# The branch around a rare path put directly behind one expert's last down products, with the next experts' rows and first weights prepared ahead of it

## The chip, the cores and the metric

The kernel runs on one core of a Trainium2 chip, in one launch. The time is device time in microseconds. The kernel before takes 2640.4 us, the median of three runs (2638.09, 2640.43, 2640.40). The engines are PE (TensorE, matrix products), DVE (VectorE), ACT (ScalarE), POOL (GpSimd) and SP (SyncE, which issues the transfers here). Each engine has its own instruction stream, and the engines wait for one another by semaphores. In the views a name with q behind it (PEldq, DVEq) stands for an engine's sequencer, which hands instructions to the engine and carries out loads of registers and branches itself.

## The reference

Two transformer blocks on 256 tokens of width 1024, in fp32, followed by a second program part of the same kind. The change touches the mixture of experts in the second layer, which is followed by a dense FFN:

```python
def moe_swiglu(h, w_router, w_gate, w_up, w_down):
    t = h.reshape(bsz * seq, d)                       # 256 x 1024
    logits = (t @ w_router).astype(jnp.float32)
    top_vals, top_idx = lax.top_k(logits, TOP_K)      # 2 of 8 experts
    top_w = jax.nn.softmax(top_vals, axis=-1)
    gates = jnp.sum(jax.nn.one_hot(top_idx, N_EXPERTS) * top_w[..., None], axis=1)
    out = jnp.zeros_like(t)
    for e in range(N_EXPERTS):
        out = out + gates[:, e:e + 1] * swiglu(t, w_gate[e], w_up[e], w_down[e])
    return out.reshape(bsz, seq, d)
```

Each expert has a gate and an up matrix of 1024 x 2816 and a down matrix of 2816 x 1024.

## The kernel before, in words

**Products.** Every fp32 matrix is split into a high and a low part: ACT casts the high part (`whi`, L156), DVE subtracts it (`wlo`, L159), each for pieces of 128 x 1024. A product is then three matmuls, high by high, high by low and low by high. Weights stream in transfers of 1 MB that SP issues (L168) into nine buffers, five named `raw` and four named `more`. There are five buffers of `whi` and four of `wlo`.

**The experts.** `moe_main` runs four experts per call. `gather` (L1260, with `xh` on ACT L1265 and `xl` on DVE L1266) picks the rows of two experts at a time: 32 matmuls with a matrix of zeros and ones (`g`, L1221). For an expert the gate and up products follow in six column blocks (L1283 to L1285), then the transposed `fh` and `fl`, then the down products in two chunks of 512 columns (L1307 to L1309; the last expert has chunks of 512, 256 and 256). A chunk's result is scaled by the row's gate into `yh` (ACT, L1311) and `yl` (DVE, L1312), and eight matmuls per 512 columns scatter it back to the tokens (L1317, L1318, "the sums" below), which DVE adds to the residual `xT` (L606). `rowwise` (L1231, L1233) makes the transposed `gt` for the sums and the gates `gr`.

**The branch.** The gathered rows hold at most 128 tokens an expert. Where one has more, `moe_rest` computes the rest in a general path, under `tc.If(n > P)` (L1211); the count `n` is loaded from `mi` (L1210). With these inputs the path is not run. The branch stands between the fourth and the fifth expert. Every engine loads the count into a register and branches by itself, and behind the branch it raises its semaphore by what the skipped path would have raised it.

**The order.** Loops emit the program, and a scheduler orders each engine's instructions by their dependencies and by estimated times, so an instruction may be moved across others of its engine, but not across the branch. Tiles of a pool are given free at its end: `p` is the pool `moe` (all of the experts), `q` is `moe_e` or `moe_f` (one call of `moe_main`). Behind the experts the FFN begins: `gg` (DVE, L556) is a product of two scales, `hl` (ACT L559, DVE L560) is the scaled `xT` in two parts, and L183 to L185 are the FFN's products. `sq` and `part` (L256, L259, L574) are for the norm.

## Time and profile before

| | |
|---|---|
| median of three runs | 2640.4 us |
| the profiled execution | 2640.62 us |
| its span | 2638.8 us |
| PE busy | 2568.5 us (97%) |
| DVE busy | 1973.1 us (75%) |
| ACT busy | 1560.9 us (59%) |
| POOL busy | 6.4 us (0%) |
| HBM read | 604.50 MB |
| mean granted clock | 0.982 |

The span runs from the first to the last instruction of the core; 1.8 us of the execution lie around it. PE is busy nearly throughout, and in the page's chain of work that ended last it holds most of the path, so what counts are the stretches in which PE stands and those in which its granted clock is at half. [...] Durations of matmuls overlap their neighbours, since they are pipelined: a matmul of 128x512 shows 0.39 us but the next one starts 0.23 us later.

### The profile page before, as it was taken

The numbers are of one execution on the slowest core, as the hardware profiler recorded it, in microseconds if no ns is written. First come the engines' busy times: TensorE is split into PE (matmuls) and PEld (weight loads), VectorE is DVE, ScalarE is ACT, GpSimd is POOL, SyncE is SP. The second block draws the span as 40 slices with busy tenths as digits, with TensorE's granted clock in tenths as the row PEclk, the third lists the DMA queues.
The fourth block names the chain that finished last, engine by engine and source line by source line (L and its number), as shares of the span: only waits on it lengthen the run. The fifth ranks groups of instructions, "written<-read, shape, count | busy, mean of one in ns | idle before, by whom it ended". The sixth has DMA issues, their size and how long they took to land.

```text
span 2638.8 us, 46342 instructions
## 1 busy us (share of the span) xinstructions
PE 2568.5 (97%) x18529; PEld 2358.6 (89%) x18529; DVE 1973.1 (75%) x3012; ACT 1560.9 (59%) x2191; POOL 6.4 (0%) x27
## 2 busy tenths in 40 slices
PE   7989998989999998999999999999999999999998
PEld 5779998978888887888878999989999999989998
DVE  5777668686999997999889765677665666677664
ACT  4444436674778876877777444675444444675443
POOL 0000000000000000000000000000000000000000
PEclk8989999998999999999999999999999999999999
DMA  9768766516999997999998557525556657525552
GB/s 310 240 219 273 266 195 224 160 65 211 350 362 350 353 378 281 345 359 348 342 362 280 175 184 218 160 65 166 186 175 193 186 176 221 155 66 175 179 181 89
DMA packets 453646, 608.62 MB, mean 231 GB/s; under 512 B 21563, under 2 KB 314448, under 8 KB 453424
## 3 DMA queue, kind: packets, MB, share of 16 engines
q1 hardware_dynamic: 453062, 605.26, 68.9%
q8 instruction: 147, 2.41, 0.4%
q0 software_dynamic: 176, 0.26, 0.1%
q14 instruction: 75, 0.61, 0.1%
q10 hardware_dynamic: 186, 0.07, 0.0%
HBM read 604.50 MB, written 1.05 MB: 229 GB/s over the span
## 4 chain that ended last, share of the span: by engine, by line
PE 59%; DVE 1%; issue 0%; ACT 0%; DVEq 0%
PE acc L183 10%; PE acc L184 10%; PE acc L185 10%; PE s L185 3%; PE s L184 3%; PE s L183 3%; PE acc L1284 3%; PE acc L1283 3%; PE acc L1285 3%; PE acc L1308 2%; PE acc L1307 1%; PE acc L1309 1%; PE s L320 1%; PE po L320 1%; PE sm L911 1%; DVE wlo L159 1%
## 5 line engine op out<-in xcount | busy, mean ns | idle before, releaser
L156 ACT CAST whi<-raw 128x1024 fp32r<-128x1024 f32 x816 | 838.4, 1038 | 710.4 <-PE acc L184 425.2
L159 DVE TENSOR_TENSOR wlo<-raw,whi 128x1024 fp32r<-128x1024 f32 x816 | 972.7, 1204 | 288.0 <-PE acc L185 202.3
L183 PE MATMUL acc<-hl,whi 128*128 128x256 f32 x2336 | 666.5, 286 | 1.9 <-ACT hl L307 1.1
L184 PE MATMUL acc<-hl,whi 128*128 128x256 f32 x2336 | 661.9, 283 | 1.7 <-DVE hl L560 0.8
L185 PE MATMUL acc<-hl,wlo 128*128 128x256 f32 x2336 | 660.5, 283 | 0.0
L183 PEld LDWEIGHTS acc<-hl,whi 128*128 128x128 f32 x2336 | 442.1, 189 | 4.9 <-ACT hl L307 1.4
L184 PEld LDWEIGHTS acc<-hl,whi 128*128 128x128 f32 x2336 | 441.9, 189 | 4.5 <-issue 1.5
L185 PEld LDWEIGHTS acc<-hl,wlo 128*128 128x128 f32 x2336 | 441.7, 189 | 0.6
L159 DVE TENSOR_TENSOR wlo<-more,whi 128x1024 fp32r<-128x1024 f32 x238 | 282.6, 1219 | 20.0 <-PE acc L1284 6.1
L1284 PE MATMUL acc<-wlo,xh 128*128 128x512 f32 (+1 forms) x768 | 288.3, 376 | 0.8
L1283 PE MATMUL acc<-whi,xh 128*128 128x512 f32 (+1 forms) x768 | 288.8, 378 | 0.0
L1285 PE MATMUL acc<-whi,xl 128*128 128x512 f32 (+1 forms) x768 | 286.0, 373 | 0.0
L156 ACT CAST whi<-more 128x1024 fp32r<-128x1024 f32 x238 | 243.7, 1047 | 42.7 <-PE acc L1285 26.9
L183 PE MATMUL s<-hl,whi 128*128 128x256 f32 x880 | 248.5, 282 | 0.0
L184 PE MATMUL s<-hl,whi 128*128 128x256 f32 x880 | 248.5, 282 | 0.0
L185 PE MATMUL s<-hl,wlo 128*128 128x256 f32 x880 | 248.4, 282 | 0.0
L1284 PEld LDWEIGHTS acc<-wlo,xh 128*128 128x128 f32 x768 | 144.4, 188 | 28.1 <-DVE wlo L159 4.5
L1283 PEld LDWEIGHTS acc<-whi,xh 128*128 128x128 f32 x768 | 144.3, 188 | 25.8
L1285 PEld LDWEIGHTS acc<-whi,xl 128*128 128x128 f32 x768 | 144.3, 188 | 25.1
L183 PEld LDWEIGHTS s<-hl,whi 128*128 128x128 f32 x880 | 166.3, 189 | 0.0
L184 PEld LDWEIGHTS s<-hl,whi 128*128 128x128 f32 x880 | 166.2, 189 | 0.0
L185 PEld LDWEIGHTS s<-hl,wlo 128*128 128x128 f32 x880 | 166.2, 189 | 0.0
(477 smaller groups left out, 4091.2 us busy)
## 6 DMA issues: line engine op xcount, KB each, us to landing
raw<-in_moe_w_gate_dram SPq DMA_DIRECT2D x50, 1024.0 KB, 7.0
raw<-in_moe_w_up_dram SPq DMA_DIRECT2D x48, 1024.0 KB, 6.7
raw<-in_ffn_wg_dram SPq DMA_DIRECT2D x44, 1024.0 KB, 5.4
raw<-in_ffn_wu_dram SPq DMA_DIRECT2D x44, 1024.0 KB, 5.4
raw<-in_moe_w_down_dram SPq DMA_DIRECT2D x42, 1024.0 KB, 6.9
more<-in_moe_w_up_dram SPq DMA_DIRECT2D x40, 1024.0 KB, 7.8
more<-in_moe_w_gate_dram SPq DMA_DIRECT2D x38, 1024.0 KB, 6.4
raw<-in_w_in_dram SPq DMA_DIRECT2D x38, 1024.0 KB, 5.3
```

The source lines that it names most:

```text
L156: i = nc.scalar.copy(hi, src[:, k0 : k0 + m])
L159: nc.vector.tensor_sub(lo, src[:, k0 : k0 + m], hi)
L183: mm(out, whi, xhi, start=first, stop=False, skip_group_check=True)
L184: mm(out, whi, xlo, start=False, stop=False, skip_group_check=True)
L185: mm(out, wlo, xhi, start=False, stop=last, skip_group_check=True)
L320: m = self.nc.tensor.matmul(o, w, x, start=start, stop=stop, skip_group_check=True)
L911: nc.tensor.transpose(ptp[:, b * P : (b + 1) * P], pe[:, b * P : (b + 1) * P], self.ident)
L1283: mm(a, xh[:, k], hi, start=k == 0, stop=False, skip_group_check=True)
L1284: mm(a, xh[:, k], lo, start=False, stop=False, skip_group_check=True)
L1285: mm(a, xl[:, k], hi, start=False, stop=k == 7, skip_group_check=True)
L1307: mm(a, fh[k], hi, start=k == 0, stop=False, skip_group_check=True)
L1308: mm(a, fh[k], lo, start=False, stop=False, skip_group_check=True)
```

## The change

The general path's branch is moved to directly behind the fourth expert's last down products: the eight sums of its second chunk (`sums`) are emitted behind the branch. `gather(4)`, which was emitted behind the branch, is emitted ahead of the fourth expert's down products, and the first two 1 MB loads of the fifth expert's gate matrix are split ahead of the branch (`self.pre`). Since these tiles are now used on both sides, `xh`, `xl`, `yh`, `yl` and `gt` come from `p` instead of `q`. The activation `tab` behind the branch is left out; the load of the count is emitted in the second expert's turn.

```diff
@@ -173,7 +174,8 @@
-            for k, (hi, lo) in enumerate(zip(*self.split(first.pop(0) if first else self.load(w, k0, nk, n0, n)))):
+            hl = self.pre.pop(0) if self.pre else self.split(first.pop(0) if first else self.load(w, k0, nk, n0, n))
+            for k, (hi, lo) in enumerate(zip(*hl)):
...
@@ -1205,14 +1207,14 @@
             split = 4
+            st = {"g": g, "rows": [], "back": [], "load": lambda: nc.values_load(mi[0:1, 0:1], min_val=0, max_val=T)}
             with tc.tile_pool(name="moe_e", bufs=1, reuse_waits="tile") as q:
-                self.moe_main(p, q, ht, pos, gates, first, 0, split, g)
-            n = nc.values_load(mi[0:1, 0:1], min_val=0, max_val=T)
-            with tc.If(n > P):
+                self.moe_main(p, q, ht, pos, gates, first, 0, split, st)
+            with tc.If(st["n"] > P):
...
@@ -1224,7 +1226,7 @@
-        gt = q.tile([P, T], dt, tag="gt", bufs=3, name=self.name("gt"))
+        gt = q.tile([P, T], dt, tag="gt", bufs=2, name=self.name("gt"))
...
@@ -1248,8 +1250,8 @@
-            xh, xl = (q.tile([P, KT, 2 * P], F32R, tag=s, bufs=1, name=self.name(s)) for s in ("xh", "xl"))
+            xh, xl = (p.tile([P, KT, 2 * P], F32R, tag=s, bufs=1, name=self.name(s)) for s in ("xh", "xl"))
...
@@ -1266,11 +1268,16 @@
-        nc.scalar.activation(q.tile([1, 1], F32, name="tab"), self.ones[:1, :1], AF.Silu)
-        g, rows = gather(e0)
-        back = []
+        if e0 == 0:
+
+            nc.scalar.activation(q.tile([1, 1], F32, name="tab"), self.ones[:1, :1], AF.Silu)
+            st["g"], st["rows"] = gather(e0)
+        else:
+            st["last"]()
+        g, rows, back = st["g"], st["rows"], st["back"]
         for e in range(e0, e1):
+            if e == 1:
+                st["n"] = st["load"]()
...
@@ -1291,13 +1298,13 @@
-                    back = [self.rowwise(q, g[:, :, b], gates, e + b, F32R) for b in range(2)]
+                    back = [self.rowwise(p, g[:, :, b], gates, e + b, F32R) for b in range(2)]
...
-            if not rows and e + 1 < e1:
+            if not rows and e + 1 < NE:
                 g, rows = gather(e + 1)
...
@@ -1307,16 +1314,25 @@
-                yh, yl = (q.tile([P, 512], F32R, tag=t, bufs=1, name=self.name(t))[:, :n] for t in ("yh", "yl"))
+                yh, yl = (p.tile([P, 512], F32R, tag=t, bufs=1, name=self.name(t))[:, :n] for t in ("yh", "yl"))
                 nc.scalar.activation(yh, a, AF.Identity, scale=gr)
                 v.scalar_tensor_tensor(yl, a, gr, yh, ALU.mult, ALU.subtract)
...
+                def sums(n0=n0, n=n, yh=yh, yl=yl, gt=gt, e=e):
...
+                if e + 1 == e1 < NE and n0:
+
+                    self.pre = [self.split(self.load(wg[e1], k0, 4, 0, 512)) for k0 in (0, 4)]
+                    st.update(g=g, rows=rows, back=back, last=sums)
+                else:
+                    sums()
...
@@ -1326,7 +1342,7 @@
-            r = q.tile([P, 8, 256], F32, tag="raw", bufs=2, name=self.name("oraw"))[:, :nk]
+            r = q.tile([P, 8, 256], F32, tag="raw", bufs=1, name=self.name("oraw"))[:, :nk]
```

PE at the branch. Of before, the rows from the fourth expert's last down product on; `s` is the result of a sum, the numbers tell tiles apart:

```order
L1309 MATMUL acc_10387<-whi_10500,fl_10243 128x512
L1317 MATMUL s_10514<-gt_8975,yh_10510 128x256 [waits Activation_49]
L1317 MATMUL s_10521<-gt_8975,yh_10510 128x256
L1318 MATMUL s_10514<-gt_8975,yl_10511 128x256 [waits DVE_49]
L1317 MATMUL s_10514<-gt_8975,yh_10510 128x256
L1318 MATMUL s_10514<-gt_8975,yl_10511 128x256
L1318 MATMUL s_10521<-gt_8975,yl_10511 128x256
L1317 MATMUL s_10521<-gt_8975,yh_10510 128x256
L1318 MATMUL s_10521<-gt_8975,yl_10511 128x256
L1210 TENSOR_LOAD mi [waits DVE_49]
L1211 COMPARE_AND_BRANCH
```

and of before, behind the not taken path:

```order
L1211 UNCONDITIONAL_BRANCH [waits PE_49]
L1260 MATMUL s_14624<-g_14617,hl_6776 128x256 [waits DVE_49]
L1260 MATMUL s_14624<-g_14617,hl_6776 128x256 x3
L1260 MATMUL s_14625<-g_14617,hl_6776 128x256 [waits DVE_49]
L1260 MATMUL s_14625<-g_14617,hl_6776 128x256 x3
```

Of after, PE's same place, with the first rows behind the path at the end:

```order
L1314 MATMUL acc_10460<-whi_10573,fh_10256 128x512
L1315 MATMUL acc_10460<-wlo_10574,fh_10256 128x512
L1316 MATMUL acc_10460<-whi_10573,fl_10257 128x512
L1210 TENSOR_LOAD mi [waits DVE_49]
L1213 COMPARE_AND_BRANCH
...
L1213 UNCONDITIONAL_BRANCH [waits PE_49]
L1326 MATMUL s_14680<-gt_8989,yh_10583 128x256 [waits DVE_49,Activation_49]
L1327 MATMUL s_14680<-gt_8989,yl_10584 128x256
L1326 MATMUL s_14680<-gt_8989,yh_10583 128x256
L1327 MATMUL s_14680<-gt_8989,yl_10584 128x256
L1290 MATMUL acc_14694<-whi_10589,xh_10265 128x512 [waits Activation_49]
```

The sums and the 32 matmuls of `gather(4)` have changed sides; behind the branch the sums come first, and the fifth expert's gate products directly behind them. The load of the count stands directly ahead of the branch in both.

DVE at the branch, of before from `yl` on:

```order
L1312 SCALAR_TENSOR_TENSOR yl_10511<-acc_10387,gr_8982,yh_10510 128x512 [waits Activation_49]
L159 TENSOR_TENSOR wlo_14702<-more_14699,whi_14701 128x1024 [waits DVE_49,DMAHW6_49,PE_49,Activation_49]
L606 SCALAR_TENSOR_TENSOR xT<-s_10514,mod_147,xT 128x256 [waits PE_49]
L606 SCALAR_TENSOR_TENSOR xT<-s_10514,mod_147,xT 128x256
L606 SCALAR_TENSOR_TENSOR xT<-s_10521,mod_147,xT 128x256 [waits PE_49]
L606 SCALAR_TENSOR_TENSOR xT<-s_10521,mod_147,xT 128x256
L159 TENSOR_TENSOR wlo_14706<-more_14699,whi_14705 128x1024 [waits DVE_49,Activation_49]
L1210 TENSOR_LOAD mi [waits DVE_49]
L1211 COMPARE_AND_BRANCH
```

and of after, with the two subtractions ahead of `yl`:

```order
L160 TENSOR_TENSOR wlo_10600<-more_10597,whi_10599 128x1024 [waits DVE_49,DMAHW6_49,PE_49,Activation_49]
L160 TENSOR_TENSOR wlo_10604<-more_10597,whi_10603 128x1024 [waits DVE_49,PE_49,Activation_49]
L1319 SCALAR_TENSOR_TENSOR yl_10584<-acc_10460,gr_8996,yh_10583 128x512 [waits Activation_49]
L1210 TENSOR_LOAD mi [waits DVE_49]
L1213 COMPARE_AND_BRANCH
```

The four additions to `xT` have gone behind the branch, and `yl` is the last instruction ahead of the load.

PE at the end of the last expert, where the FFN starts. Of before, from the last two down products on:

```order
L1308 MATMUL acc_18234<-wlo_18310,fh_17973 128x256
L1309 MATMUL acc_18234<-whi_18309,fl_17974 128x256
L183 MATMUL acc_18437<-hl_18347,whi_18440 128x256 [waits Activation_49]
L184 MATMUL acc_18437<-hl_18348,whi_18440 128x256 [waits DVE_49]
L185 MATMUL acc_18437<-hl_18347,wlo_18441 128x256
L183 MATMUL acc_18437<-hl_18347,whi_18440 128x256
...
L1317 MATMUL s_18335<-gt_16706,yh_18331 128x256 [waits Activation_49]
```

Of after:

```order
L1315 MATMUL acc_18232<-wlo_18308,fh_17971 128x256
L1316 MATMUL acc_18232<-whi_18307,fl_17972 128x256
L1326 MATMUL s_18333<-gt_16704,yh_18329 128x256 [waits Activation_49]
L1327 MATMUL s_18333<-gt_16704,yl_18330 128x256 [waits DVE_49]
L1326 MATMUL s_18333<-gt_16704,yh_18329 128x256
L1327 MATMUL s_18333<-gt_16704,yl_18330 128x256
L251 MATMUL sm_18384<-ones,part_18109 128x1 [waits DVE_49,PE_49]
L251 MATMUL sm_18384<-ones,part_18109 128x1
L185 MATMUL acc_18435<-hl_18345,whi_18438 128x256 [waits Activation_49]
L185 MATMUL s_18494<-hl_18345,whi_18497 128x256
```

Before, 25 FFN products stand between the last down product and the first of the last four sums. Now the sums come first, then two matmuls for the norm (L251), and the FFN's first product behind them.

ACT at the same place. Of before:

```order
L156 CAST whi_18444<-raw_18438 128x1024 [waits DVE_49,PE_49]
L559 ACTIVATE hl_18347<-xT,gg 128x256 [waits DVE_49,Activation_49]
L559 ACTIVATE hl_18347<-xT,gg 128x256 x3
L559 ACTIVATE hl_18347<-xT,gg 128x256 [waits DVE_49]
L156 CAST whi_18499<-raw_18497 128x1024 [waits DMAHW6_49,PE_49]
L156 CAST whi_18503<-raw_18497 128x1024 [waits PE_49,Activation_49]
L1311 ACTIVATE yh_18331<-acc_18234,gr_16713 128x256 [waits PE_49]
L256 ACTIVATE sq_18231<-xT 128x512 [waits DVE_49]
L559 ACTIVATE hl_18347<-xT,gg 128x256
```

Of after:

```order
L157 CAST whi_18497<-raw_18495 128x1024 [waits DMAHW6_49,DVE_49,PE_49]
L157 CAST whi_18501<-raw_18495 128x1024 [waits DVE_49,PE_49]
L1318 ACTIVATE yh_18329<-acc_18232,gr_16711 128x256 [waits PE_49]
L258 ACTIVATE sq_18229<-xT 128x512 [waits DVE_49]
L576 ACTIVATE sq_18372<-xT,colsb 128x256 x2
L157 CAST whi_18564<-raw_18562 128x1024 [waits DMAHW7_49,Activation_49]
L576 ACTIVATE sq_18376<-xT,colsb 128x256 [waits DVE_49]
L576 ACTIVATE sq_18376<-xT,colsb 128x256
L576 ACTIVATE part_18369<-xT,colsb 128x256 x2
L561 ACTIVATE hl_18345<-xT,gg 128x256 [waits DVE_49]
L561 ACTIVATE hl_18345<-xT,gg 128x256 x7
```

Before, the first five `hl` stand ahead of the last two casts and of the last `yh`. Now all eight stand behind them, behind `sq`, behind another cast and behind six activations of L576 (L574 before). On DVE `gg`, which `hl` reads, has likewise gone from ahead of the first FFN weights' subtraction to behind the last additions to `xT`.

## Rows read from the trace of the kernel before

**Rows 1.** Windows: stretch, length, busy by engine (PE, PEld, DVE, ACT, POOL), clock, DMA share, GB/s

```profile
1060.00:1440.00 380.00, 379.06 (x1888) 316.10 (x1887) 346.26 (x356) 288.67 (x327) 0.00 (x0) 1.00 0.99 345
```

**Rows 2.** Timeline of PE at the branch; start, duration, instruction, idle before and releaser

```profile
1032.56 0.40 PE L1309 MATMUL acc<-whi,fl 128*128 128x512 f32 x1
1033.74 0.50 PE L1317 MATMUL s<-gt,yh 128*128 128x256 f32 x2 [0.78 <-ACT yh L1311]
1034.52 0.38 PE L1318 MATMUL s<-gt,yl 128*128 128x256 f32 x1 [0.29 <-DVE yl L1312]
...
1035.22 0.28 PE L1318 MATMUL s<-gt,yl 128*128 128x256 f32 x1
1041.62 5.49 PE L1260 MATMUL s<-g,hl 128*128 128x256 f32 x24 [6.12 <-DVEq L1211]
```

**Rows 3.** Timeline of DVE at the branch

```profile
1033.72 0.75 DVE L1312 SCALAR_TENSOR_TENSOR yl<-acc,gr,yh 128x512 fp32r<-128x512 f32 x1 [1.41 <-ACT yh L1311]
1035.79 1.65 DVE L606 SCALAR_TENSOR_TENSOR xT<-s,mod,xT 128x256 f32<-128x256 f32 x4
```

**Rows 4.** Instructions of L1210, the load of the count: durations in ns, starts

```profile
L1210 PEldq TENSOR_LOAD <-mi x1: 484/484/484, 1034.5 to 1034.5; - x1
L1210 DVEq TENSOR_LOAD <-mi x1: 547/547/547, 1035.7 to 1035.7; - x1
```

**Rows 5.** Instructions of L1211, the branch: durations in ns, starts

```profile
L1211 POOLq EVENT_SEMAPHORE  x4: 17/42/43, 646.4 to 646.7; - x4
L1211 POOLq COMPARE_BRANCH  x1: 45/45/45, 642.5 to 642.5; - x1
...
L1211 PEldq COMPARE_BRANCH  x1: 6212/6212/6212, 1035.1 to 1035.1; - x1
L1211 DVEq COMPARE_BRANCH  x1: 72/72/72, 1036.3 to 1036.3; - x1
...
L1211 DVEq EVENT_SEMAPHORE  x1: 21/21/21, 1041.5 to 1041.5; - x1
```

**Rows 6.** Windows that begin with PE's resumption behind a gap, and the FFN's start

```profile
1041.62:1050.00 8.38, 8.38 (x45) 8.12 (x45) 3.37 (x8) 2.83 (x7) 0.00 (x0) 0.67 0.19 72
417.76:427.00 9.24, 9.24 (x57) 9.14 (x58) 7.93 (x24) 5.91 (x8) 0.00 (x0) 0.74 0.37 123
385.44:400.00 14.56, 14.56 (x87) 14.45 (x88) 11.38 (x22) 6.06 (x11) 0.00 (x0) 0.67 0.38 115
1440.00:1450.00 10.00, 9.17 (x77) 8.97 (x77) 9.72 (x16) 8.72 (x16) 0.00 (x0) 1.00 0.72 211
```

**Rows 7.** Timeline of PE, the first instruction behind two gaps

```profile
385.44 0.98 PE L287 MATMUL sm<-dg,ones 128*128 128x128 f32 x3 [2.69 <-DVE dg L286]
417.76 0.55 PE L183 MATMUL acc<-g,whi 128*128 128x256 f32 x1 [5.04 <-DVE bc L940]
```

**Rows 8.** Timeline of PE at the start of the FFN

```profile
1440.17 0.28 PE L1309 MATMUL acc<-whi,fl 128*128 128x256 f32 x1
1440.29 0.28 PE L183 MATMUL acc<-hl,whi 128*128 128x256 f32 x1
1441.39 0.39 PE L184 MATMUL acc<-hl,whi 128*128 128x256 f32 x1 [0.83 <-DVE hl L560]
```

**Rows 9.** Timeline of ACT at the start of the FFN

```profile
1440.00 1.98 ACT L156 CAST whi<-raw 128x1024 fp32r<-128x1024 f32 x2
1441.89 0.46 ACT L1311 ACTIVATE yh<-acc,gr 128x256 fp32r<-128x256 f32 x1
1442.25 0.61 ACT L256 ACTIVATE sq<-xT 128x512 f32<-128x512 f32 x1
1442.77 0.49 ACT L559 ACTIVATE hl<-xT,gg 128x256 fp32r<-128x256 f32 x1
1443.17 0.89 ACT L574 ACTIVATE sq<-xT,colsb 128x256 f32<-128x256 f32 x2
1443.97 1.98 ACT L156 CAST whi<-raw 128x1024 fp32r<-128x1024 f32 x2
```

## The prediction

> **What bounds the kernel now.** I read the windows of the experts first. Between 1060 and 1440 us PE works 379.06 of 380.00 us at full clock, while DVE works 346 and ACT 289 [rows 1]. So PE is the bound, and work moved between places where PE is fed changes nothing. What can change the time is a stretch in which PE stands, or runs at half clock. The PE timeline, read next, shows such a stretch at the branch.

> The last down product of the fourth expert begins at 1032.56 and ends at T = 1032.96 [rows 2]. PE waits for `yh` and `yl`, does the eight sums until 1035.50, and then stands 6.12 us until 1041.62 [rows 2]. From T to the resumption that is 8.66 us, of which the sums are eight steps of 0.116 us, 0.93 us (256 columns; the FFN rows 1440.17 and 1440.29 are one such step apart [rows 8]). So 7.73 us are lost, and a clock loss comes on top: the 8.38 us behind the resumption have a mean granted clock of 0.67, so 0.33 x 8.38 = 2.8 us [rows 6].

> What the wait is made of stands in the rows of L1210 and L1211. DVE's sequencer loads the count at 1035.7 (547 ns), which is just behind the end of the last sum at 1035.50, for which DVE's last two additions to `xT` wait. It compares at 1036.3, and the first event behind the branch comes at 1041.5 [rows 2 to 5]. PE's sequencer loads at 1034.5, when its last wait, that for `yl`, is met, and its branch holds it for 6212 ns from 1035.1 to about 1041.3 [rows 4, 5]. PE's first matmul is released by DVE's sequencer [rows 2]. So the chain is: the last wait ahead of an engine's branch is met, load and compare take 0.6 us, some 5.2 us pass before the next instruction, in sum 5.8 us on DVE. The sequencer doesn't wait for its engine: DVE's four additions run until 1037.44 [rows 3] while its sequencer is at the branch.

> **The change at the branch.** The sums and their additions are now behind the branch. DVE's last wait ahead of it is that of `yl` for `yh`. With the durations of before `yl` could start at 1033.72, T + 0.76 [rows 3]. The load then begins at T + 0.8 instead of T + 2.75, and with the same 5.8 us the event comes at T + 6.6 and PE resumes at T + 6.7 (before, 0.1 us lay between them). PE's own sequencer has its last wait ahead of T and ends its 6.7 us (484 ns and 6212 ns) at or before T + 6.7. All of PE's work that lay in the gap is now behind it: lost are 6.7 us instead of 7.73, a gain of 1.0 us.

> How long the 5.2 us are is not fixed. POOL's own branch shows 3.9 us (642.5 to 646.4) and PE's 6.2 [rows 5]. With 3.9 the resumption is at T + 5.4, a gain of 2.3, with 6.2 at T + 7.7, which is no gain. I take 5.2, DVE's own. [...]

> The gather's 32 matmuls move ahead of the branch into a stretch with no room on PE; they cost there what they no longer cost behind it. Before, 24 of them ran at half clock (5.49 us [rows 2]). Now the sums and the first gate products, which come behind the resumption, take that place, so the clock loss of 2.8 us stays as it is. The casts and subtractions of the first two loads (four pieces, 24 matmuls of 512 columns, twice 0.116 us each, 5.5 us) are a stock on which PE lives while ACT and DVE start again. The five `whi` buffers and the four of `wlo` were filled ahead of the branch before as well, by the scheduler. The load of the count stands directly ahead of the branch in both orders, so its earlier place in the text does nothing, and the dropped `tab` (0.20 us on ACT) was on no path. I cost these at nothing, since DVE has 9% and ACT 24% of free time in the experts [rows 1]; without that cover the gather's work on ACT and DVE would show as waits of PE ahead of T.

> **The change at the FFN.** The order shows a second difference, far from the branch. At the end of the eighth expert, 25 FFN products used to fill the time in which the last `yh` and `yl` are made. PE stood there for 0.83 us only, and the clock stayed at 1.00 [rows 6, 8]. Now PE has the sums, two small matmuls and then the FFN's first product, which waits for the first `hl`, and on ACT that stands behind much else.

> I follow ACT from T2 = 1440.45, the end of the last down product [rows 8], with the starts of before as the price of each step [rows 9]. The last cast ahead of `yh` needs a `whi` buffer that six matmuls from the end comes free, at T2 - 0.7; it takes 1.05 us (half of the pair's 1.98, plus its tail), so `yh` starts at T2 + 0.4. `yh` takes 0.36 until `sq` can start, `sq` 0.52, the first two L576 0.80, a cast 0.95, two more pairs of L576 0.80 each. That is 0.4 + 0.36 + 0.52 + 0.8 + 0.95 + 1.6 = 4.6, and `hl` takes 0.49, so it is done at T2 + 5.1. PE can start at 5.15. Of this the four sums are 0.47 us of work, so PE stands 4.7 us where it stood 0.83. **The loss is 3.85 us.** DVE's `gg` comes ahead of that: it is behind a subtraction, `yl`, two adds and two additions to `xT`, by about T2 + 3.8 as I estimate from a subtraction's 1.2 us and `yl`'s 0.75 at twice the width.

> A gap of that size was followed by half clock elsewhere. Behind the gap of 5.04 us at 417.76 the mean clock of the next 9.24 us was 0.74, so 2.4 us were lost; behind that of 2.69 us at 385.44 it was 0.67 over 14.56 us, so 4.8 us [rows 6, 7]. The lower end is nothing, as behind the 0.83 us [rows 6, 8]. I take 2.4, from the gap that is nearest in length.

> **The sum.** -1.0 at the branch, +3.85 and +2.4 at the FFN: +5.2 us. The profiled execution took 2640.62 us (a span of 2638.8 and 1.8 around it), 0.2 us above the median of 2640.4. So 2645.8 by the first and 2645.6 by the second; I predict 2645.6.

> **The rivals.**
> - *The clock holds at the FFN.* The 4.7 us are not one gap: four sums and two small matmuls lie in them. Then the time is 2640.4 - 1.0 + 3.85 = 2643.2. Against it: the 2.69 us gap was enough for a fall [rows 6, 7].
> - *The FFN's start is covered.* If ACT comes to its last casts earlier than I have it (in after it has five fewer `hl`, 2 us, to do ahead of them), `hl` could be early enough to hide most of the gap: at most the branch's gain is left, 2640.4 - 1.0 = 2639.4, or 2638.1 with the short branch. Against it: the buffers of `whi`, not ACT, hold those casts back, and the order forbids `hl` to pass them.
> - *The price is the full one, clearly slower.* The clock stays at half as long as behind 385.44, and the branch is as long as PE's own: 2640.4 + 0 + 3.85 + 4.8 = 2649.1. It decides if the FFN's first 9 us or so run at half. For it: of the two gaps measured the shorter one had the longer stretch [rows 6, 7].
> [...]
> [...]

> **How the numbers follow.** A difference under 0.2% (5.3 us) can't be told from none in a measurement of this kernel; the bounds are 2635.1 and 2645.7. The forecast has a chance of 0.50 with an own range of 2643.5 to 2647.5, and lies astride the upper bound: 0.26 of it within, 0.24 above. The clock that holds: 0.18, within. The covered start: 0.10, within. The full price: 0.15, above. Faster: 0.07, near the lower bound, of which 0.04 below it. So faster 0.04, the same 0.57, slower 0.39. The range of 2638.5 to 2650 leaves out the fast case and a part of the covered one, and takes in the upper ends of the clock and the branch.

> **What would show it.** In the trace after: DVE's sequencer loading the count some 0.8 us behind the last down product, and PE resuming 6.7 us behind it, with the sums first; a clock at half for some 5 us from there on, as before; no waits of PE in the fifth expert's gate products. At the FFN: PE idle for 4 to 5 us ahead of the first product of L185, released by `hl` of ACT (L561), and half clock behind it. The prediction is wrong if PE is fed there in under 2 us, if the branch's rows shorten by more than 2.5 us, or if new waits of PE show up in the experts.

## The result: slower by 0.53%, and the profile after

The changed kernel takes 2654.19 us (median of five runs, 2650.82 to 2658.46) against 2640.1 us (five runs). The ratio is 1.0053 with a 95% interval of 1.0043 to 1.0064, so 14 us slower; 2645.6 was forecast. The profiled execution took 2653.55 us with a span of 2651.4, which is 12.6 us over the span before.

The windows of the changed kernel, one of the experts as in [rows 1], one from PE's resumption at the branch, and one from the FFN's first product; the columns are those of [rows 1]:

```profile
1060.00:1440.00 380.00, 379.40 (x1854) 313.41 (x1853) 343.04 (x357) 285.69 (x319) 0.00 (x0) 1.00 0.98 342
1049.93:1058.00 8.07, 8.07 (x31) 6.81 (x32) 5.20 (x7) 2.94 (x3) 0.00 (x0) 0.75 0.08 24
1453.50:1462.00 8.50, 8.40 (x60) 8.39 (x61) 5.74 (x13) 5.21 (x12) 0.00 (x0) 0.81 0.29 93
```

In the experts PE is busy as before, at full clock (1.00). Its time looks the same, but it does less in it: 1854 matmuls in 380 us against 1888 (part of that is that the windows cover other instructions). So the steps themselves must be looked at. PE's timeline, the first and the last of 47 matmuls of 512 columns in a row, in the third expert's gate and up products, of the kernel before (in these rows the first name behind the arrow, `wlo`, is the moving operand and the second, `xh`, the stationary one, which PEld loads ahead of the matmul: the 128x128 load for the first of them runs 0.19 us from 859.74):

```profile
859.97 0.39 PE L1284 MATMUL acc<-wlo,xh 128*128 128x512 f32 x1
...
870.52 0.39 PE L1285 MATMUL acc<-whi,xl 128*128 128x512 f32 x1
```

and of the changed kernel:

```profile
863.01 0.40 PE L1291 MATMUL acc<-wlo,xh 128*128 128x512 f32 x1
...
873.74 0.39 PE L1292 MATMUL acc<-whi,xl 128*128 128x512 f32 x1
```

A step is the time from one matmul's start to the next one's. Before, 46 steps take 10.55 us, 0.2293 each; after, 10.73 us, 0.2333 each. Nothing waits there, no clock is below full, and the durations shown (0.39, 0.40) hardly tell. Over the experts' products, 512-column steps have these means (in us, all of them at full clock):

| | before | after |
|---|---|---|
| gate and up, all experts | 0.2294 | 0.2334 |
| down, experts 1 to 4 | 0.2299 | 0.2333 |
| down, experts 5 to 8 | 0.2297 | 0.2283 |

PE at the branch, after; the fence answers to [rows 2]:

```profile
1041.78 0.40 PE L1316 MATMUL acc<-whi,fl 128*128 128x512 f32 x1
1049.93 0.55 PE L1326 MATMUL s<-gt,yh 128*128 128x256 f32 x1 [7.75 <-DVEq L1213]
...
1051.56 0.41 PE L1327 MATMUL s<-gt,yl 128*128 128x256 f32 x1
1051.77 0.63 PE L1290 MATMUL acc<-whi,xh 128*128 128x512 f32 x1
```

The last down product ends at T = 1042.18, PE resumes at 1049.93, 7.75 us later, and the eight sums come behind it. Before, 8.66 us less 0.93 of sums were lost, 7.73. So the branch costs what it did. The loads of the count and the branches, after, which answer to [rows 4, 5]:

```profile
L1210 PEldq TENSOR_LOAD <-mi x1: 484/484/484, 1037.8 to 1037.8; - x1
L1210 DVEq TENSOR_LOAD <-mi x1: 545/545/545, 1042.9 to 1042.9; - x1
```

```profile
L1213 PEldq COMPARE_BRANCH  x1: 6233/6233/6233, 1038.4 to 1038.4; - x1
L1213 ACTq COMPARE_BRANCH  x1: 45/45/45, 1042.8 to 1042.8; - x1
L1213 DVEq COMPARE_BRANCH  x1: 72/72/72, 1043.6 to 1043.6; - x1
L1213 ACTq EVENT_SEMAPHORE  x1: 17/17/17, 1043.9 to 1043.9; - x1
...
L1213 PEldq EVENT_SEMAPHORE  x1: 51/51/51, 1044.7 to 1044.7; - x1
L1213 DVEq EVENT_SEMAPHORE  x1: 21/21/21, 1049.8 to 1049.8; - x1
```

DVE loads 0.76 us behind T, as forecast. But from its compare to its event 6.2 us pass, not 5.2. ACT needs 1.0 us where it had needed 5.2. PE's own branch starts 3.8 us ahead of T and is over at 1044.7, so DVE's is the one that PE waits for.

The FFN's start, first PE, which answers to [rows 8], then ACT, to [rows 9]:

```profile
1447.54 0.28 PE L1316 MATMUL acc<-whi,fl 128*128 128x256 f32 x1
1448.61 0.38 PE L1326 MATMUL s<-gt,yh 128*128 128x256 f32 x1 [0.79 <-ACT yh L1318]
1450.87 0.58 PE L1327 MATMUL s<-gt,yl 128*128 128x256 f32 x1 [1.88 <-DVE yl L1319]
...
1453.60 0.58 PE L185 MATMUL acc<-hl,whi 128*128 128x256 f32 x1 [0.60 <-ACT hl L561]
```

```profile
1447.14 1.05 ACT L157 CAST whi<-raw 128x1024 fp32r<-128x1024 f32 x1 [0.74 <-PE acc L1316]
1448.09 0.47 ACT L1318 ACTIVATE yh<-acc,gr 128x256 fp32r<-128x256 f32 x1
...
1451.44 0.91 ACT L576 ACTIVATE sq<-xT,colsb 128x256 f32<-128x256 f32 x2 [0.64 <-DVE part L261]
1452.26 0.89 ACT L576 ACTIVATE part<-xT,colsb 128x256 f32<-128x256 f32 x2
1453.06 3.29 ACT L561 ACTIVATE hl<-xT,gg 128x256 fp32r<-128x256 f32 x8
```

The first FFN product starts 5.78 us behind the last down product's end at 1447.82 (5.15 forecast), released by ACT's first `hl`. The 0.63 us more are about what ACT waits for DVE's `part` (0.64), which the forecast did not have. The half clock behind it (0.50 in windows of 1 us from 1453.60 to 1456.60, 0.81 over the 8.50 us of the third window) is 1.6 us.

**Where the 12.6 us are.** From start to start, summed over PE's matmuls between the first gate product and the last down product, and behind it:

| part | after less before, us |
|---|---|
| gate, up and down products, steps | +10.9 |
| the gather's matmuls (now at full clock, 1.00 from 940 to 1042) | -2.5 |
| the sums (now partly at half clock, 0.50 from 1050 to 1053) | +1.0 |
| steps over 0.45 us (waits), the branch's included | -1.7 |
| transposes and the row-wise matmuls | -0.4 |
| first 400 matmuls behind the last down product (53.8 against 48.6) | +5.2 |
| all the rest | +0.1 |

Of the 10.9 about 1 us is half clock that lay on the gather before. Some 10 us are longer steps, most of the loss, and the prediction had no such term.

### The profile page after: what moved, and what is told of

Same layout as the page of the kernel before. It is cut to its first block, busy times and chain, and to the rows that moved or that the text cites. A ratio compares the mean times of both kernels' runs of the same rounds, so it can differ in the third digit from the quotient of the medians.

```text
span 2651.4 us, 46351 instructions
## 1 busy us (share of the span) xinstructions
PE 2582.9 (97%) x18529; PEld 2364.4 (89%) x18529; DVE 1973.7 (74%) x3012; ACT 1562.6 (59%) x2190; POOL 6.4 (0%) x27
## 3 DMA queue, kind: packets, MB, share of 16 engines
HBM read 604.50 MB, written 1.05 MB: 228 GB/s over the span
## 4 chain that ended last, share of the span: by engine, by line
PE 59%; DVE 1%; ACT 0%; issue 0%; DVEq 0%
PE acc L185 10%; PE acc L186 10%; PE acc L187 9%; PE s L187 3%; PE s L186 3%; PE s L185 3%; PE acc L1291 3%; PE acc L1290 3%; PE acc L1292 3%; PE acc L1315 2%; PE acc L1314 2%; PE acc L1316 1%; PE s L322 1%; PE po L322 1%; PE sm L913 1%; DVE wlo L160 1%
## 5 line engine op out<-in xcount | busy, mean ns | idle before, releaser
L185 PE MATMUL acc<-hl,whi 128*128 128x256 f32 x2336 | 668.0, 286 | 1.9 <-ACT hl L309 1.1
L185 PEld LDWEIGHTS acc<-hl,whi 128*128 128x128 f32 x2336 | 443.1, 190 | 4.9 <-ACT hl L309 1.4
L157 ACT CAST whi<-more 128x1024 fp32r<-128x1024 f32 x238 | 244.5, 1048 | 60.3 <-PE acc L1292 37.9
L185 PE MATMUL s<-hl,whi 128*128 128x256 f32 x880 | 248.9, 283 | 0.0
L185 PEld LDWEIGHTS s<-hl,whi 128*128 128x128 f32 x880 | 166.8, 190 | 0.0
```

What stands on the lines that cost most here:

```text
L157: i = nc.scalar.copy(hi, src[:, k0 : k0 + m])
L185: mm(out, whi, xhi, start=first, stop=False, skip_group_check=True)
```

## The experiments

One thing that differs between the kernels in that stretch without touching an instruction is where the tiles lie. The built programs have the addresses: `xh` begins at byte 176352 of a partition before and 176320 after, `fh` at 196832 before, after at 203072 in the first call and at 203040 in the second (`tab`, 32 bytes with its padding, is only in the first). The split weights stay: `whi` begins at 76064 and `wlo` at 96544, both in steps of 4096. In the experts' products `xh`, `xl`, `fh`, `fl` are stationary, the weights move. All the comparisons are with the kernel before in runs on the same chip.

**Place alone, in the changed kernel (e1).** Instructions and order are the same on every engine.

```diff
+            p.tile([1, 1], F32, name="pad")          # first call, ahead of xh
             st["g"], st["rows"] = gather(e0)
         else:
+            q.tile([1, 1], F32, name="padf")         # second call, ahead of s and fh
             st["last"]()
```

> The changed kernel with 32 unused bytes ahead of xh and another 32 in the second call's pool, so that xh begins at byte 176352 of a partition instead of 176320 and fh at 203104; every instruction and its order are as in the changed kernel. Theory (place): PE's step of a 512-column matmul depends on whether its stationary tile begins at a multiple of 64 bytes; the gate products' mean step falls from 0.2334 to about 0.229 us, the down products' of experts 0 to 3 from 0.2333 to 0.229, and the time by 7 to 10 us to about 2645. Rival (order): the longer step comes from the new order or from the other engines' work beside it; then the step stays at 0.233 and the time at 2654.

2650.2 us, ratio 1.0038 (1.0026 to 1.0051); 1.0053 without the pads. The 47 matmuls of the third expert's gate and up products:

```profile
867.46 0.39 PE L1293 MATMUL acc<-wlo,xh 128*128 128x512 f32 x1
...
878.00 0.39 PE L1294 MATMUL acc<-whi,xl 128*128 128x512 f32 x1
```

46 steps in 10.54 us, 0.2291: the gate's long step is gone with 32 bytes. But `fh`, at 203104 now, has 0.2332 in the first call and 0.2334 in the second, where it had 0.2283, so a multiple of 64 isn't the rule, and part of the gain is lost: 1920 gate and up steps x 4.1 ns = 7.9 us less, and 462 down steps x 5.1 ns = 2.4 us more. That is 5.5 us net, where 7 to 10 were expected; by the medians 14.1 us over the kernel before became 10.9.

**The FFN's order alone (e2).** The shared tiles are in a pool of their own, at the same addresses.

```diff
+            sh = c.enter_context(tc.tile_pool(name="moe_x", bufs=1, reuse_waits="tile"))
-            st = {"g": g, ...
+            st = {"x": sh, "g": g, ...
-            xh, xl = (p.tile(
+            xh, xl = (st["x"].tile(       # yh, yl, gt, gr likewise
```

> The changed kernel with xh, xl, yh, yl, gt and gr in a pool of their own that lies at the same addresses as before, so that the FFN's first tiles overlap no pool that holds them. The order at the start of the FFN is that of the kernel before again (25 FFN products ahead of the last sums), the rest is as in the changed kernel. Theory (place, and FFN order apart): PE's wait at the FFN's start and the half clock behind it go, the steps stay long: 5 to 6 us faster than the changed kernel, about 2648.5. Rival (one cause: the FFN's start costs little): under 2 us faster.

2649.1 us, ratio 1.0036 (1.0023 to 1.0049). PE's only wait over 0.1 us at the FFN's start (engine, line, releaser; total, times, longest us):

```profile
PE acc L186 <- DVE hl L562: 0.7, 1, 0.7
```

The order is again that of the kernel before, the first 400 matmuls behind the last down product take 48.6 us as before, and the steps are long as in the changed kernel. So what moved `gg` and `hl` is the pool that the shared tiles belong to, and not their addresses. My reading is that the scheduler puts a tile that opens a region behind the last use of every pool that held the region, and that with `yl` and `gt` in `moe` this last use came later; no other run tests that rule.

**Both (e3).**

> Both edits: the pool of their own and the 32 bytes. Theory: the two gains add up, 13 us off the changed kernel, 2640 to 2641, what is left against the kernel before is the branch alone, a difference within 2 us. Rival: the branch's place itself costs more than its trace shows, and the time stays over 2645.

2645.6 us, ratio 1.0023 (1.0013 to 1.0034). The two gains add up (14.1 - 3.2 - 4.3 gives 6.6 over the kernel before, 6.2 measured), but the down products' step of 0.2333 stays in it, which the expectation had not. By the time alone the rival could stand (over 2645, since the branch's place costs more than its trace shows); e5 and e6 decide between the two.

**Place alone, in the kernel before (e4).** Unused bytes ahead of `xh`, 32 in the first call, 64 in the second; instructions and order as before.

```diff
+        for k in range(2 if e0 else 1):
+            q.tile([1, 1], F32, name=self.name("pad"))
         g, rows = gather(e0)
```

> The kernel before with 32 unused bytes ahead of xh in the first call of the experts (xh at byte 176384, fh at 196864, both multiples of 64) and 64 bytes in the second (176416 and 196896, both 32 past one); instructions and order as in the kernel before. Theory (place): experts 0 to 3 take the long step, 0.233 us, experts 4 to 7 stay at 0.227 to 0.229; 5 to 7 us slower than the kernel before, about 2646. Rival (order): both halves stay at 0.229 and the time at 2640.

2643.0 us, ratio 1.0013 (1.0004 to 1.0021). Experts 1 to 4 have steps of 0.2331 (gate) and 0.2333 (down), experts 5 to 8 0.2281 and 0.2278. Both halves are as the place theory said; from the steps 960 x 3.8 ns + 528 x 3.4 ns - 960 x 1.4 ns - 462 x 1.9 ns = 3.2 us, and 3.6 were measured. The 5 to 7 us expected were too many, since the second half became faster instead of staying as it was. The order rival falls.

**The good place in both (e5, e6).** `xh` at 176416 in both; `fh` at 203296 in e5 (on e2's pools), at 196896 in e6 (the kernel before with 64 unused bytes in each call).

> The changed kernel with the pool of its own for the shared tiles, and unused bytes so that xh begins at byte 176416 and fh at 203296 in both calls, both 32 past a multiple of 256, as in the fast half of the shifted kernel before. Theory (the step goes by the stationary tile's place within 256 bytes, 32 is fast): all 512-column steps of the experts at 0.228 us; against the version with both edits 0.0013 x 1920 and 0.005 x 1000, 7 us faster, about 2638. Rival (the step goes by whether the place is a multiple of 64): the gate products' step stays at 0.2293, the down products' falls to it, 2642.

> The kernel before, order unchanged, with 64 unused bytes ahead of xh in both calls: xh at 176416, fh at 196896, 32 past a multiple of 256. Theory (place): steps of 0.228 instead of 0.2293 and 0.2298, so 1.3 ns x 1920 and 1.9 ns x 1000, about 4 us faster than the kernel before, 2635.5. What the aligned changed kernel takes more or less than this one is the branch and nothing else: between -1 and +2 us. Rival (the place matters only where it is bad): 2639.5, as before.

2634.8 us, ratio 0.9979 (0.9970 to 0.9988), and 2635.9 us, ratio 0.9985 (0.9976 to 0.9994). The same 47 matmuls in e6:

```profile
860.52 0.39 PE L1286 MATMUL acc<-wlo,xh 128*128 128x512 f32 x1
...
870.95 0.39 PE L1287 MATMUL acc<-whi,xl 128*128 128x512 f32 x1
```

46 steps in 10.43 us, 0.2267. The means are 0.2276 to 0.2282 in both. e6 is 4.6 us under the kernel before, as expected (about 4). e5 came out lower than expected (2638): by the ratios it is 0.44%, 11.6 us, under e3, where 7 were expected and 8.4 follow from the steps measured; the intervals of the two are too wide to tell these apart. What is left between the two kernels is the branch's place: 1.2 us, with intervals that overlap, so no difference that these runs can tell. PE's wait at the branch in e5 and in e6 (there behind the sums):

```profile
PE s L1333 <- DVEq L1214: 8.0, 1, 8.0
```

```profile
PE s L1260 <- PEq L1211: 6.0, 1, 6.0
```

**Place or distance (e7).** On e6: the stationary tiles of the experts stay, the moving ones are moved by 32 bytes.

```diff
+        if not self.padded:
+            self.padded = self.pw.tile([1, 1], F32, name="padw")
         for s, b in (("whi", self.nhi), ("wlo", self.nlo)):
```

> The same as the aligned kernel before, but with 32 unused bytes ahead of the split weights too, so that the moving tiles begin at 64 instead of 32 past a multiple of 256, with the stationary ones left where they are (the experts' tiles at the same bytes). Theory (the stationary tile's own place decides): the experts' steps stay at 0.228 us. Rival (the distance between the stationary and the moving tile decides): at this distance, 32 bytes, the step was 0.233 in the runs so far, and should be so here in all the experts, some 14 us longer in the span. The FFN's products, whose stationary tiles are the split weights, will show their own step at the new place.

```profile
859.78 0.39 PE L1289 MATMUL acc<-wlo,xh 128*128 128x512 f32 x1
...
870.50 0.39 PE L1290 MATMUL acc<-whi,xl 128*128 128x512 f32 x1
```

46 steps in 10.72 us, 0.2330; the mean is 0.2332 in all the experts. The one execution took 2647.2 us, 11 over e6's median, where some 14 were expected. My theory of the stationary tile's own place falls, the rival holds: the distance between the two decides.

**A branch that DVE reaches early (e8).** On e5; the fourth expert's last chunk is copied out by ACT, `yh` and `yl` are made from the copy behind the branch.

```diff
+                    y = p.tile([P, 2048], F32, tag="more", bufs=4, ...)[:, :n]
+                    nc.scalar.activation(y, a, AF.Identity, scale=gr)
...
+                    if y is not None:                # in sums(), behind the branch
+                        nc.scalar.copy(yh, y)
+                        v.tensor_sub(yl, y, yh)
...
-                    self.pre = [... for k0 in (0, 4)]
+                    self.pre = [... for k0 in (0,)]
```

> The aligned changed kernel with the fourth expert's last chunk copied out of its accumulator by ACT ahead of the branch, and yh and yl made from that copy behind it, so that DVE's last wait ahead of the branch is that of a subtraction some 6 us ahead of the last down product; one load instead of two is named to be split ahead, and the order shows the splits behind the branch. Theory (DVE's 6.9 us of load, compare and fetch begin at its last wait): DVE is through its branch within 1.5 us of the last down product, PE resumes when its own or ACT's branch ends, 2.5 to 4 us behind it instead of 7.8, 3 to 5 us faster than the aligned changed kernel. [...]

The 6.9 us are those from DVE's load to its event (1042.9 to 1049.8 in the changed kernel); that a part of them is a fetch was the author's reading, which no run shows.

2632.9 us, ratio 0.9967 (0.9956 to 0.9977), 1.9 us under e5, with intervals that just overlap. The branch in e8, where the last down product ends at 1032.23:

```profile
L1214 DVEq COMPARE_BRANCH  x1: 72/72/72, 1027.3 to 1027.3; - x1
L1214 PEldq COMPARE_BRANCH  x1: 6723/6723/6723, 1028.7 to 1028.7; - x1
L1214 DVEq EVENT_SEMAPHORE  x1: 21/21/21, 1033.0 to 1033.0; - x1
L1214 ACTq COMPARE_BRANCH  x1: 45/45/45, 1033.1 to 1033.1; - x1
L1214 PEldq EVENT_SEMAPHORE  x1: 51/51/51, 1035.5 to 1035.5; - x1
L1214 ACTq EVENT_SEMAPHORE  x1: 17/17/17, 1038.4 to 1038.4; - x1
```

```profile
PE po L1234 <- PEq L1214: 3.5, 1, 3.5
PE s L1341 <- ACT yh L1335: 2.1, 1, 2.1
```

DVE is through 0.7 us behind the last down product, and PE resumes at 1035.74, 3.5 us behind it, held by its own branch. So the theory of when the wait begins holds. Less comes of it than expected: PE's first work is small matmuls of the new pair and then a wait of 2.1 us for `yh`, since ACT's branch takes 5.3 us here (1.0 in the changed kernel), and the mean clock from the resumption to 1052.00 is 0.60 over 16.26 us, in e5 0.76 over 11.33 us.

**The same rule in the FFN (e9).** On e8, with 64 unused bytes ahead of the FFN's `hl`.

```diff
+        for t in range(2):
+            k.p2.tile([1, 1], F32, name=k.name("pad"))
         k.h2 = k.hilo(k.p2, KT)
```

> The version with the early branch, with 64 unused bytes ahead of the FFN's hl tiles (124384 instead of 124320 and so on; the tiles behind move by 64 as well), order and instructions unchanged. Theory (PE's step is a function of the distance between stationary and moving tile within 256 bytes): 5766 products of 256 columns go from a distance of 128, 0.1189 us, to 64, for which the shifted kernels' last chunks showed 0.1150: 22 us less; 1584 go from 96 to 32 (0.1174 to 0.1183, 1.4 us more) and 528 from 32 to 224 (0.1183 to 0.1167, 0.8 us less): in sum 22 us faster, about 2611. Rival (the distance matters for the experts' products alone, or DVE and ACT bound the FFN as soon as PE is quicker): under 5 us faster.

2612.0 us against 2643.3 on that chip, ratio 0.9884 (0.9868 to 0.9900). The FFN's products, 63 matmuls of 256 columns in a row, first and last, before and in e9:

```profile
1499.88 0.28 PE L184 MATMUL s<-hl,whi 128*128 128x256 f32 x1
...
1507.23 0.28 PE L183 MATMUL acc<-hl,whi 128*128 128x256 f32 x1
```

```profile
1499.82 0.28 PE L186 MATMUL s<-hl,whi 128*128 128x256 f32 x1
...
1506.84 0.28 PE L185 MATMUL s<-hl,whi 128*128 128x256 f32 x1
```

62 steps take 7.35 us before and 7.02 in e9, 0.1185 and 0.1132. Relative to e8 the ratio falls by 0.83%, 22 us, as expected from the distance alone.

**No branch (e10).** e6 without the load of the count, the branch and the general path, which these inputs don't run.

> The aligned kernel before without the branch: the count is not loaded, and the general path, which these inputs don't run, is left out of the program. Theory: the 7.7 us that PE stands between the last down product and its resumption, less some 1 us for yh and yl, and the half clock of 5 us behind it go: 8 to 10 us faster than the aligned kernel before, about 2627. Rival (the branch's wait hides work that would be waited for anyway): under 4 us.

2630.5 us, ratio 0.9951 (0.9937 to 0.9965). PE at that place, from the last down product to the first gate product of the next expert:

```profile
1031.58 0.39 PE L1307 MATMUL acc<-whi,fl 128*128 128x512 f32 x1
1032.75 0.51 PE L1315 MATMUL s<-gt,yh 128*128 128x256 f32 x2 [0.78 <-ACT yh L1309]
...
1034.62 0.28 PE L1316 MATMUL s<-gt,yl 128*128 128x256 f32 x1
1035.09 0.50 PE L1281 MATMUL acc<-whi,xh 128*128 128x512 f32 x1 [0.19 <-ACT xh L1261]
```

The waits left are those for `yh` (0.78 us) and for `xh` (0.19). Against e6's ratio that is 0.34%, 9 us, some 4 us either way by the two intervals: the whole price of the branch in the order of the kernel before. For the changed order no such run was made; e5 and e6, which differ by 1.2 us, suggest the same price.

## Why the prediction was wrong

- **What bounds the kernel.** PE does, as said. The failed step is what the prediction drew from it: "work moved between places where PE is fed changes nothing", and only "a stretch in which PE stands, or runs at half clock" can change the time. It took the time of a matmul on a fed PE at full clock as fixed, as does the part on the time before ("what counts are the stretches in which PE stands and those in which its granted clock is at half"). The tiles' new pools had no term in the sum, but another pool means another address, and PE's step depends on it: 0.2294 us became 0.2334 in the gate and up products. This term, left at nothing without a reason, measured some 10 us.
- **The branch.** Forecast -1.0 us, with 0 and -2.3 as bounds. DVE's load came when forecast (T + 0.76); the compare to the event took 6.2 us instead of 5.2, so the bound of no gain is right. That bound was PE's own 6.2 us, and it was DVE's branch that PE waited for, so that the two figures agree is luck. In the eleven profiles with a branch DVE's value goes with the program: 5.0 to 5.3 us in the four with the order of before (before, e4, e6, e7), 6.1 to 6.4 in the five with the change's (after, e1, e2, e3, e5), 5.6 and 5.2 in the two with the early one (e8, e9). Within one order the value differs by up to 0.4 us, and between the first two groups by about 0.8 us at least, so noise from run to run does not make the difference between before and after; what does, no run shows. Between DVE's compare and its event the DMA view has four packets of the kind `instruction` (on q8 and q14), before (1036.3 to 1041.5) and after (1043.6 to 1049.8); in the 380 us from 1060 to 1440 it has 26 in each of the two kernels. Which engine they are for, and whether its branch waits for them, the view does not show. That DVE's 5.2 us would stay the same with other work around the branch was the author's estimate.
- **The clock at the branch.** Forecast unchanged, 2.8 us. The window behind the resumption has 0.75 over 8.07 us, 2.0 us. In windows of 1 us the clock shows 0.50 from 1042 to 1047 before and from 1050 to 1053 after, and it is 1.00 from 1048 to 1058 and from 1054 to 1058.
- **The gather and the splits.** Forecast as costing nothing where they moved to; no new waits of PE show in the experts. Right.
- **The FFN's start.** Forecast +3.85 and +2.4, measured +5.2 in both together; the first product came 5.78 us behind the last down product (5.15 forecast), with 1.6 us of clock. The mechanism was right, the late `hl` with half clock behind it, and e2 shows that the loss goes when the order goes back.
- **The rivals.** None had the places. The range ended at 2650, since it was built from the terms that I had and left no room for a term that I had not.

One sentence ahead of the prediction is wrong too: the scheduler does move instructions across the branch. The splits for the fifth expert, emitted behind it before, stand ahead of it there, and in e8 those emitted ahead stand behind.

## What to carry to other kernels

When tiles change pools, or a pool before them gains or loses even a 32-byte tile, compare the addresses of the built programs, and measure matmuls from start to start in a stretch without waits: neither busy shares nor the durations of single rows (here 0.39 and 0.40 us) show a step that is 2% longer (0.2293 and 0.2333). Where the order of a distant stage changes, ask which pool's end its first tiles wait for. And the branch here cost from the last wait ahead of it on the engine that came through last (PE resumed 7.75 us behind the last down product in the changed kernel, 3.5 in e8), so what helped (e8: 1.9 us by the medians, with intervals that just overlap) was to let that engine arrive early, not to put work on the other side of it.

## What the runs showed of the hardware

| stationary less moving, mod 256 | 512 columns | 256 columns |
|---|---|---|
| 0 | 0.2278 (13111) | 0.1197 (2526) |
| 32 | 0.2333 (1018) | 0.1183 (8623) |
| 64 | 0.2332 (1897) | 0.1142 (5750) |
| 96 | none | 0.1174 (17067) |
| 128 | 0.2319 (187) | 0.1189 (91509) |
| 160 | 0.2334 (3537) | 0.1198 (2762) |
| 192 | 0.2294 (6264) | 0.1170 (1392) |
| 224 | 0.2332 (4146) | 0.1168 (6040) |

It is the distance and not either place: 224 at 512 columns comes from the places 0 and 32 (e4) and 32 and 64 (e7), with 0.2332 each; 128 at 256 columns from four pairs, with 0.1185 to 0.1189. The best distance is another one for 512 columns (0) than for 256 (64). In e5 `xh` lies 0 and `fh` 256 bytes from the moving tile within 512, and both are fast, so 256 is the period as far as these two tell. Why it is so, no run shows.

The other surprise is ACT's branch: 1.0 us from compare to event in the five kernels with the change's order and 5.2 to 5.4 in the six others that have a branch, with the same skipped path.
